# Layer step: the first two projection blocks loaded into tiles not yet in use, key gathers booked and issued differently, the sample's output rows laid out as 128 half rows

## The chip, the cores and the metric

One Trainium2 chip, one of its cores. The metric is the device time of one execution in microseconds (us), median of the runs shown. A profile of one execution lists what each engine did: PE (TensorE, the matmuls), DVE (VectorE), ACT (ScalarE), POOL (GpSimd), and SP, which here issues nearly all DMAs. Each engine works through its own queue in order.

## The reference

One decoder layer for a prompt of 256 tokens and for 8 sample requests of 8 tokens each, 320 rows in all, width 2048. One input projection feeds three branches: sparse attention over the top keys that an indexer chooses, a gated linear recurrence, and cross-attention into a memory.

```
z = einsum('btd,dn->btn', h, w)                      # 8272 columns, split into the branches' parts
dots = einsum('bthd,bld->bthl', iq, ik) * 64 ** -0.5     # 16 index heads of 64
sc = einsum('bth,bthl->btl', iw * 16 ** -0.5, relu(dots))
_, sel = top_k(where(causal, sc, -inf), n_sel)       # 64 keys (prompt) or 256 (sample)
a = softmax over the selected keys, times their values, times silu(gate)
y = layernorm(ALPHA * x + cat(a, b, m) @ w_out) * ln_g + ln_b
```

For the sample, past keys and values lie in pages (16 of 128 tokens per request, found through a page table): index keys `cache_idx_k`, keys `cache_k` and values `cache_v`.

## The kernel before

**Projection.** x stands transposed as 16 slabs (k) of 128 x 320. Every product is done at more than single precision: an operand is cast to a short format (`hi`, on ACT) and the remainder (`lo`, on DVE or POOL) is kept, and three matmuls are added: hi·hi, hi·lo, lo·hi. A block is 128 output columns: 48 matmuls of 320 columns into one PSUM tile `pj` (two buffers). The blocks come in the order of `PROJECTIONS`: `ikw` (the index key and head weights, 80 columns), eight `iq` (index queries, two heads each), eight `aq`, `ak`, `av`, then the rest. A weight block is loaded in two halves (list `wspec`; `half` counts them), each 128 x 1024 numbers, into the ring `wr` of three buffers (`load_w`); `prep` makes `wh` and `wl` of it (two buffers each); `pe_quantum` issues the matmuls, six per k. The blocks ikw and iq0 are cut into four parts each and taken in turns, ikw, iq0, ikw, iq0. x arrives in six loads (`load_x`, 2, 2, 2, 2, 4, 4 slabs) between those weights, and `split_x` makes `xh` and `xl`.

**After a block** its function empties the accumulator: `ev_ikw` (a DVE shuffle and multiplies with the rotary tables `tabi`, an ACT copy of the head weights), `ev_iq(i)` through `rope` (shuffle, multiply on DVE, a second multiply and an addition by `TT`). `TT` gives an operation to DVE or POOL, whichever the builder's clock says ends it earlier.

**Order of work.** A builder (`Plan`, `Engine`) keeps a clock for each engine and for the DMAs, with a cost for each operation, while it writes the program. The main loop asks that clock which weights to load, which operand to prepare, and whether PE gets a piece of projection, a page unit or a background step; each engine's queue is thereby fixed when the program is built. In `Plan.dma` a gather on POOL's queue costs 0.1 + 1.04 us, and other transfers run at 360 GB/s.

**Background steps.** `setup` loads `pidx` (row numbers), the page table and `tabi`, and makes `poff`. `idx_load` then gathers the index keys of all pages with 64 indirect DMAs on POOL, 16 for each of four groups of requests, into tiles tagged `pg`, `S`, `pg`, `S`; before every second one it waits until POOL is booked less than 0.5 us ahead. `idx_head` copies the eight new index keys per request (`nk`) on POOL. `idx_prompt` scores the prompt: for each iq block eight matmuls of 64 rows (`t,t` in the trace), relu on ACT, sums on DVE. `idx_sample` does the same for the sample with the gathered keys (from iq7 on), then `topk_sample` picks the keys in 32 rounds. `soft`, `unit` (page units: two requests, two pages each, of K or V), `hgrn`, `cross_prompt` and `split` follow. Page loads may start once `half` is over 38.

**End.** The output projection works on 512-column chunks n for row groups m = 0, 1 (prompt) and 2 (the 64 sample rows). `out_chunk` adds x and gathers row statistics, and after the last chunk `finish(m)` normalises: for each chunk subtract and multiply with g (DVE), then scale (ACT) and add b (POOL), or, for the sample's last two chunks, both in one DVE operation; two stores of 1024 columns.

Of the kernel before, what the change touches and what calls it, by code (L numbers as in the profile page):

```python
# [25 lines left out]
NS, NT = 64, 320  # L26
# [15 lines left out]
class Plan:  # L42
# [154 lines left out]
def hymba_step(ctx: ExitStack, tc: tile.TileContext, I, O):  # L197
# [95 lines left out]
    qpad = new([128, 8, 8, 32], "qpad")  # L293
# [76 lines left out]
    def ev_aq(h):  # L370
        def f(ps):
            x, sh = rope(ps, False)
            AQ[h] = T(256)
            r = h // 4 * 16 + h % 2 * 8
            TT(OP.add, qpad[:, :, h, r:r + 8], x[:, 256:320].rearrange("p (b t) -> p b t", b=8),
               sh[:, 256:320].rearrange("p (b t) -> p b t", b=8))
# [100 lines left out]
    def add_block(kind, i):  # L477
        nk = 4 if (kind, i) in (("ikw", 0), ("iq", 0)) else 8
        if kind == "ikw":
            add_T(I["wik"], ev_ikw, 80, nk)  # L480
        elif kind == "mem":
            for k in range(16):
                wspec.append(dict(kind="mem", k=k, n=1024, nq=1, src=I["wm"][:, k, :]))
        else:
            base, ev = {"iq": (32, ev_iq), "aq": (0, ev_aq), "ak": (8, ev_ak), "av": (16, ev_av), "mq": (56, ev_mq),
                        "bf": (44, None), "bq": (40, None), "bi": (48, None), "g": (24, None)}[kind]
            if kind == "g":
                add_T(wt[24 + i if i < 8 else 44 + i if i < 12 else 48 + i], ev_gate(i, i % 4 == 3))
            else:
                add_T(wt[base + i], ev(i) if ev else ev_b((kind, i)), nk=nk)  # L490
# [10 lines left out]
    wspec[0:8] = [wspec[4 * (i % 2) + i // 2] for i in range(8)]  # L501
# [37 lines left out]
    def load_w(i):  # L539
        s = wspec[i]  # L540
        WR[i] = new([128, 1024], "wr")
# [7 lines left out]
    def prep(i):  # L549
# [6 lines left out]
        if s.get("res") and kept.index(i) >= RES - 4:  # L556
# [5 lines left out]
            hi, lo = spare_w.pop(0), spare_w.pop(0)  # L562
        elif s.get("acc") == "rest":
# [5 lines left out]
        if i < 44:  # L569
# [34 lines left out]
    def unit(n):  # L604
        kind, p, u = punits[n]
        tl = [PG.pop((n, b)) for b in range(2)]
        if kind == "K":
# [5 lines left out]
            for hh in range(2):  # L613
                for h2 in range(2):
                    for b, hp, g in GROUPS:
                        h = 4 * hh + 2 * hp + h2
                        PE.matmul(st["kv"][g:g + 32, c:c + 256], qpad[:, 2 * p + b, h, :],
# [98 lines left out]
    def idx_head():  # L716
# [266 lines left out]
    def soft(p):  # L983
        yield from wait(("K", p), "topk", ("ak", 7), "masks")
        yield need(akS, qpad, ps=0)
# [4 lines left out]
        for hh in range(2):  # L990
            for h2 in range(2):
                for b, hp, g in GROUPS:
                    h = 4 * hh + 2 * hp + h2
                    PE.matmul(ps[g:g + 32, :], qpad[:, 2 * p + b, h, :], akS[:, h, :], start=hh == h2 == 0,
# [360 lines left out]
    def pe_quantum(i, q):  # L1355
# [5 lines left out]
        if s["kind"] == "T":  # L1361
# [106 lines left out]
    def out_chunk(n, ms, acc):  # L1468
        wait = acc == "main" and n in DEFER

        def f(o):
            c = slice(512 * n, 512 * n + 512)
            bn = st["bn"]
            for m, ps in zip(ms, o):
# [12 lines left out]
                r = st["r", 2][:, c]  # L1487
# [14 lines left out]
    def finish(m):  # L1502

        g, b = st["gb"]
        rows = 128 if m < 2 else 64
        r = st["r", m]
        s = T8()[0:rows]
        DVE.bn_aggr(out=s[:, 0:2], in_=st["bn"][0:rows, m])
        ACT.activation(s[:, 2:3], s[:, 1:2], AF.Sqrt, bias=eps[0:rows, 1:2])
        for c in range(4):  # L1510
            cs = slice(512 * c, 512 * c + 512)
            DVE.scalar_tensor_tensor(r[:, cs], r[:, cs], s[:, 0:1], g[0:rows, cs], op0=OP.subtract, op1=OP.mult)
            if c == 0:
                DVE.reciprocal(s[:, 2:3], s[:, 2:3])
            if m < 2 or c < 2:
                ACT.activation(r[:, cs], r[:, cs], AF.Copy, scale=s[:, 2:3])
                POOL.tensor_add(r[:, cs], r[:, cs], b[0:rows, cs])
            else:
                DVE.scalar_tensor_tensor(r[:, cs], r[:, cs], s[:, 2:3], b[0:rows, cs], op0=OP.mult, op1=OP.add)
            if c % 2:  # L1520
                SP.dma_start(O["y"][128 * m:128 * m + rows, 512 * c - 512:512 * c + 512],
                             r[:, 512 * c - 512:512 * c + 512])


    def load_x(k0, n, tag="pg"):
        t = new([128, n, NT], tag)
        SP.dma_start(t, I["xT"][:, k0:k0 + n, :])
        return k0, n, t

    def split_x(k0, n, t, mid=None):  # L1530
        for a in range(0, n, 2):
            if a and mid:
                mid()
            k = slice(k0 + a, k0 + a + 2)
            ACT.copy(xh[:, k, :], t[:, a:a + 2, :])
            DVE.tensor_sub(xl[:, k, :], t[:, a:a + 2, :], xh[:, k, :].bitcast(F32))
        free(t)

    load_w(0)
# [5 lines left out]
    first = [load_x(0, 2, "bp"), load_x(2, 2, "bp")]  # L1545
    load_w(1)
    first += [load_x(4, 2), load_x(6, 2)]
    load_w(2)
    prep(0)
    load_w(3)  # L1550
    split_x(*first[0])
    split_x(*first[1])
    first.append(load_x(8, 4))
    prep(1)
    load_w(4)
    split_x(*first[2])
    split_x(*first[3])
    first.append(load_x(12, 4))
    prep(2)
    load_w(5)  # L1560
    prep(3)
    split_x(*first[4], mid=lambda: prep(4))
    split_x(*first[5])
    first.clear()

    def setup():
        SP.dma_start(pidx, I["pidx"])
        SP.dma_start(ptab, I["pt"])
        for j in range(2):
            SP.dma_start(tabi[j], I["tabi"][:, j, :])  # L1570
# [12 lines left out]
        POOL.memset(qpad, 0.0)  # L1583
        POOL.memset(avS[0:64], 0.0)
# [4 lines left out]
        done.add("setup")  # L1589

# [32 lines left out]
    nw, npg, nunit, half, quarter, nprep = 6, 0, 0, 0, 0, 5  # L1623
# [23 lines left out]
    def loads():  # L1647
        nonlocal nw, npg
        while True:
# [16 lines left out]
            if (half > 38 and n < len(punits) and len(PG) + ("q" in st) + ci_live(0) < BUFS["pg"] and n <= nunit + 2  # L1666
# [30 lines left out]
    while half < len(wspec) or bg or outq or pending or nunit < len(punits):  # L1697
# [3 lines left out]
        while nprep < nw and nprep <= half + 1 + rest_next and prep_ready(nprep):  # L1701
# [143 lines left out]
```

## Time and profile before

| | before |
|---|---|
| median of 3 runs | 940.07 us (939.50 to 940.48) |
| the profiled execution's own time | 940.44 us |
| its span, first to last instruction | 938.7 us |
| mean granted TensorE clock | 0.984 |
| PE busy | 892.1 us, 95% |
| DMA traffic | 265.54 MB, mean 283 GB/s |
| index-key gathers on POOL | 64 (32 into `pg`, 32 into `S`) |

Line 127 is the one line in `Engine` through which nearly every operation is recorded, so groups are told apart by the tiles they write and read: `pj<-xh,wh` is a projection matmul, `wl<-wr,wh` a weight remainder, `t<-t,t` the work on rotated tiles, `pg<-in_ci,poff` a gather. A timeline row is: start, duration, engine, line, operation, output<-inputs, shapes, count, and in brackets the idle time before it with what ended it. A row of a table of windows is: the window, its length, then for PE, PEld (weight loads), DVE, ACT and POOL the busy time and in brackets the instructions, the granted clock, the DMA share and GB/s. In the list of waits a row is: who waited <- for whom: total us, times, longest.

### The profile page before, as it was taken

To read this page: it belongs to the slowest core of one execution; us is meant where nothing else is said; L and a number is where in the kernel's file an instruction comes from. 1 tells how busy PE (TensorE), PEld (TensorE's weight loads), DVE (VectorE), ACT (ScalarE), POOL (GpSimd) and SP (SyncE) were. 2 spreads that over 40 slices of the span, in tenths; PEclk is the share of its full clock that TensorE was granted. 3 is DMA by queue.
4 is the path that set the end of the run, shared out by engine and by line. 5 is a ranking of instruction groups with operands and counts; after the bars stand their busy time and mean duration, and the time that the engine had idled before them with its cause. 6 is when DMAs were issued, how large, how long until landed. Compare 5 with 4: busy or idle time off the path is not lost. (4 is left out here: it accounts for less than half of the span.)

```text
span 938.7 us, 18269 instructions
## 1 busy us (share of the span) xinstructions
PE 892.1 (95%) x6590; PEld 743.1 (79%) x6590; DVE 579.3 (62%) x1096; ACT 385.1 (41%) x673; POOL 299.8 (32%) x265
## 2 busy tenths in 40 slices
PE   8878899999999999999999999999999999999993
PEld 7777787888888888778888787777798878688872
DVE  5655799658899973376775763565444322645567
ACT  4322465644334344234354243444344332633333
POOL 1688783215565420032431231355100010011016
PEclk9999999999999999999999999999999999999997
DMA  8534443399899997997989989999898999945633
GB/s 257 190 117 157 125 128 120 96 343 372 273 375 348 361 360 271 406 347 287 365 330 339 408 311 376 402 342 400 320 326 322 358 353 404 303 143 155 202 113 112
DMA packets 79646, 265.54 MB, mean 283 GB/s; under 512 B 10050, under 2 KB 16899, under 8 KB 78979
## 3 DMA queue, kind: packets, MB, share of 16 engines
q1 hardware_dynamic: 77506, 260.17, 76.4%
q0 software_dynamic: 2048, 4.20, 1.5%
q8 instruction: 52, 0.85, 0.4%
q14 instruction: 40, 0.32, 0.1%
HBM read 255.60 MB, written 8.73 MB: 282 GB/s over the span
## 5 line engine op out<-in xcount | busy, mean ns | idle before, releaser
L127 PE MATMUL pj<-xh,wh 128*128 128x320 f32 (+1 forms) x1040 | 337.1, 324 | 6.7 <-ACT t L127 6.3
L127 PE MATMUL pj<-xh,wl 128*128 128x320 f32 (+1 forms) x1040 | 323.7, 311 | 1.8 <-DVE wl L127 1.8
L127 PE MATMUL pj<-xl,wh 128*128 128x320 f32 (+1 forms) x1040 | 323.8, 311 | 0.9 <-DVE xl L127 0.9
L127 DVE TENSOR_TENSOR wl<-wr,wh 128x1024 fp32r<-128x1024 f32 (+2 forms) x143 | 176.4, 1234 | 225.5 <-ACT wh L127 219.4
L127 ACT CAST wh<-wr 128x1024 fp32r<-128x1024 f32 (+2 forms) x178 | 181.7, 1022 | 237.2 <-PE pj L127 187.1
L127 PEld LDWEIGHTS pj<-xh,wh 128*128 128x128 f32 (+1 forms) x1040 | 197.0, 189 | 36.7 <-issue 25.9
L127 PEld LDWEIGHTS pj<-xh,wl 128*128 128x128 f32 (+1 forms) x1040 | 196.9, 189 | 3.0 <-DVE wl L127 2.9
L127 PEld LDWEIGHTS pj<-xl,wh 128*128 128x128 f32 (+1 forms) x1040 | 197.2, 190 | 2.5 <-DVE xl L127 1.4
L127 POOL TENSOR_TENSOR wl<-wr,wh 128x1024 fp32r<-128x1024 f32 x35 | 85.8, 2450 | 286.0 <-ACT wh L127 283.6
L127 POOL TENSOR_TENSOR t<-t,t 128x320 f32<-128x320 f32 (+4 forms) x74 | 66.0, 893 | 124.9 <-ACT t L127 89.9
L127 ACT ACTIVATE t<-t 128x320 f32<-128x320 f32 (+1 forms) x68 | 29.3, 455 | 79.5 <-DVE t L127 77.6
L127 PE MATMUL kv<-pg,qpad 128*32 128x256 f32 x1024 | 59.8, 381 | 0.0
L127 PE MATMUL va<-pg,PT 128*32 128x512 f32 x512 | 59.3, 596 | 0.0
L127 PEld LDWEIGHTS kv<-pg,qpad 128*32 128x32 f32 x1024 | 31.0, 110 | 23.0 <-issue 2.7
L127 POOL DMA_INDIRECT pg<-in_ci,poff x32 | 38.6, 1205 | 26.6 <-DMA t<-in_tabi 18.4
L127 DVE TENSOR_TENSOR t<-t,t 128x128 f32<-128x128 f32 (+5 forms) x50 | 23.9, 479 | 37.3 <-POOL t L127 21.8
L127 POOL DMA_INDIRECT S<-in_ci,poff x32 | 38.2, 1195 | 9.0 <-issue 8.4
L127 DVE MAX8 PT<-PT 128x8 f32<-128x1032 f32 x32 | 39.3, 1229 | 0.4
L127 DVE MATCH_REPLACE8 PT<-PT 128x1032 f32<-128x1032 f32 x32 | 39.0, 1218 | 0.0
L127 PEld LDWEIGHTS va<-pg,PT 128*32 128x32 f32 x512 | 14.5, 109 | 30.3 <-issue 27.8
L127 PE MATMUL mB<-t,t 128*128 128x64 f32 (+5 forms) x140 | 23.7, 328 | 9.9 <-DVE t L127 8.1
L127 POOL TENSOR_TENSOR t<-t,tabm 128x320 f32<-128x320 f32 x16 | 14.0, 876 | 56.2 <-DVE t L127 52.2
(294 smaller groups left out, 1240.2 us busy)
## 6 DMA issues: line engine op xcount, KB each, us to landing
pg<-in_ck SPq DMA_DIRECT2D x128, 512.0 KB
pg<-in_cv SPq DMA_DIRECT2D x128, 512.0 KB
wr<-in_wt SPq DMA_DIRECT2D x126, 512.0 KB
wr<-in_wo SPq DMA_DIRECT2D x36, 512.0 KB
wr<-in_wm SPq DMA_DIRECT2D x16, 512.0 KB
pg<-in_cXK SPq DMA_DIRECT2D x8, 512.0 KB
pg<-in_cXV SPq DMA_DIRECT2D x8, 512.0 KB
bp<-in_st SPq DMA_DIRECT2D x4, 512.0 KB
```

What stands on the lines that cost most here:

```text
L127: res = f(*a, **k)
```

## The change

The first two blocks are cut into eight parts each (two k, one part of six matmuls per turn), but loaded in four pieces each (four k) into parts of two tiles tagged `S`; their `hi` and `lo` go into the tiles tagged `PT`, `qpad`, `cat1` (`stacked`) and `pg`, all not otherwise used at that time. x comes as eight loads of two slabs into three `pg` tiles, in turns with the weights, and the two halves of iq1 are issued right behind; `tabi` is loaded before `pidx`. `qpad` is allocated and cleared, and `avS` cleared, only after iq0 is done. The builder's clock books a gather at 0.1 + 1.35 us and transfers at 270 GB/s up to 7 us and 375 afterwards; `idx_load` goes on when POOL is booked less than 1.5 us ahead. The eight `nk` copies move from POOL to ACT. Since the first blocks have eight more parts, the counts 38 and 44 become 46 and 52. For the sample, rows 0 to 63 of a 128 x 1024 tile hold the first 1024 columns and rows 64 to 127 the other 1024, with g and b loaded to match; statistics of the upper half are copied down, mean and factor copied up, and four DVE operations and four stores do what six DVE, two ACT and two POOL operations and two stores did.

```diff
         else:
-            self.t[q] = t + 1.04
+            self.t[q] = t + 1.35
             t += 2.6
-        self.t["DMA"] = end = max(self.t["DMA"], t) + nbytes / 360e3
+        self.t["DMA"] = end = max(self.t["DMA"], t, 0.9) + nbytes / (375e3 if t > 7 else 270e3)
...
-    qpad = new([128, 8, 8, 32], "qpad")
...
-        nk = 4 if (kind, i) in (("ikw", 0), ("iq", 0)) else 8
+        nk = 2 if (kind, i) in (("ikw", 0), ("iq", 0)) else 8
...
-    wspec[0:8] = [wspec[4 * (i % 2) + i // 2] for i in range(8)]
+    wspec[0:16] = [wspec[8 * (i % 2) + i // 2] for i in range(16)]
...
-        WR[i] = new([128, 1024], "wr")
+        WR[i] = s["home"] if "home" in s else new([128, 1024], "wr")
...
+        elif "pair" in s:
+            hi, lo = s["pair"]
...
-        if i < 44:
+        if i < 52:
             DVE.tensor_sub(lo[:, 0:n], raw[:, 0:n], hi[:, 0:n].bitcast(F32))
...
-                    yield from idle("POOL", 0.5)
+                    yield from idle("POOL", 1.5)
...
-                    POOL.tensor_copy(nk[64 * j:64 * j + 64, 8 * a:8 * a + 8],
+                    ACT.copy(nk[64 * j:64 * j + 64, 8 * a:8 * a + 8],
                                      ik[64 * j:64 * j + 64, 256 + 8 * b:264 + 8 * b])
...
-                PE.matmul(ps, h3[:, k, :], xh[:, K, :], start=K == 0, stop=False)
-                PE.matmul(ps, h3[:, k, :], xl[:, K, :], start=False, stop=False)
-                PE.matmul(ps, l3[:, k, :], xh[:, K, :], start=False, stop=K == 15)
+                j = k + s.get("sub", 0)
+                PE.matmul(ps, h3[:, j, :], xh[:, K, :], start=K == 0, stop=False)
+                PE.matmul(ps, h3[:, j, :], xl[:, K, :], start=False, stop=False)
+                PE.matmul(ps, l3[:, j, :], xh[:, K, :], start=False, stop=K == 15)
...
-        rows = 128 if m < 2 else 64
-        r = new([128, 2048], "S" if m < 2 else "pg")[0:rows]
-        SP.dma_start(r, I["xn"][128 * m:128 * m + rows, :])
-        st["r", m] = r
+        if m < 2:
+            st["r", m] = r = new([128, 2048], "S")
+            SP.dma_start(r, I["xn"][128 * m:128 * m + 128, :])
+        else:
+            st["r", 2] = r = new([128, 1024], "pg")
+            st["gb2"] = gb = new([128, 2, 1024], "pg")
+            for h in range(2):
+                rows, cols = slice(64 * h, 64 * h + 64), slice(1024 * h, 1024 * h + 1024)
+                SP.dma_start(r[rows], I["xn"][256:320, cols])
+                for j, n in enumerate(("lng", "lnb")):
+                    SP.dma_start(gb[rows, j, :], bass.AP(tensor=I[n].tensor, offset=I[n].offset + 1024 * h,
+                                                         ap=[[0, 64], [1, 1024]]))
...
-                r = st["r", 2][:, c]
+                rows = slice(64 * (n // 2), 64 * (n // 2) + 64)
+                r = st["r", 2][rows, 512 * (n % 2):512 * (n % 2) + 512]
                 DVE.scalar_tensor_tensor(r, r, ALPHA, ps[0:64], op0=OP.mult, op1=OP.add)
                 DVE.tensor_add(r, r, ps[64:128])
                 if acc == "rest":
                     DVE.tensor_add(r, r, part(n))
-                DVE.bn_stats(out=bn[0:64, 2, n, :], in_=r)
+                DVE.bn_stats(out=bn[rows, 2, n, :], in_=r)
                 if n == 3:
-                    finish(2)
+                    finish_sample()
...
-            if m < 2 or c < 2:
-                ACT.activation(r[:, cs], r[:, cs], AF.Copy, scale=s[:, 2:3])
-                POOL.tensor_add(r[:, cs], r[:, cs], b[0:rows, cs])
-            else:
-                DVE.scalar_tensor_tensor(r[:, cs], r[:, cs], s[:, 2:3], b[0:rows, cs], op0=OP.mult, op1=OP.add)
+            ACT.activation(r[:, cs], r[:, cs], AF.Copy, scale=s[:, 2:3])
+            POOL.tensor_add(r[:, cs], r[:, cs], b[:, cs])
...
+    def finish_sample():
+        r, gb, bn, s = st["r", 2], st["gb2"], st["bn"], T8()
+        DVE.tensor_copy(bn[0:64, 2, 2:4, :], bn[64:128, 2, 2:4, :])
+        DVE.bn_aggr(out=s[0:64, 0:2], in_=bn[0:64, 2])
+        ACT.activation(s[0:64, 2:3], s[0:64, 1:2], AF.Sqrt, bias=eps[0:64, 1:2])
+        DVE.tensor_copy(s[64:128, 0:1], s[0:64, 0:1])
+        for c in range(2):
+            cs = slice(512 * c, 512 * c + 512)
+            DVE.scalar_tensor_tensor(r[:, cs], r[:, cs], s[:, 0:1], gb[:, 0, cs], op0=OP.subtract, op1=OP.mult)
+            if c == 0:
+                DVE.reciprocal(s[0:64, 2:3], s[0:64, 2:3])
+                DVE.tensor_copy(s[64:128, 2:3], s[0:64, 2:3])
+        for c in range(2):
+            cs = slice(512 * c, 512 * c + 512)
+            DVE.scalar_tensor_tensor(r[:, cs], r[:, cs], s[:, 2:3], gb[:, 1, cs], op0=OP.mult, op1=OP.add)
+            for h in range(2):
+                SP.dma_start(O["y"][256:320, 1024 * h + 512 * c:1024 * h + 512 * c + 512], r[64 * h:64 * h + 64, cs])
+    raws = [new([128, 1280], "S"), new([128, 2048], "S")]
+    his = [new([128, 2320], "PT", F32R), new([128, 2048], "qpad", F32R)]
+    los = [stacked, new([128, 2048], "pg", F32R)]
+    xs = [new([128, 6, NT], "pg") for _ in range(3)]
+    plan.split.update(t.tensor.name for t in raws + his + los + xs)
+    for i in range(16):
+        w = (320, 512)[i % 2]
+        c = slice(w * (i // 4), w * (i // 4 + 1))
+        wspec[i].update(n=w, home=raws[i % 2][:, c], pair=(his[i % 2][:, c], los[i % 2][:, c]), sub=i // 2 % 2 * 2)
+    def load_first(i):
+        k = slice(4 * (i // 4), 4 * (i // 4) + 4)
+        src = (I["wik"], wt[32])[i % 2][:, k, :]
+        WR[i] = wspec[i]["home"]
+        SP.dma_start(WR[i], src.rearrange("p a c -> p (a c)"))
+    def prep_first(i):
+        prep(i)
+        WH[i + 2], WL[i + 2] = WH[i], WL[i]
+    def x_pair(a):
+        return xs[a // 3][:, 2 * (a % 3):2 * (a % 3) + 2, :]
+    def load_x(a):
+        SP.dma_start(x_pair(a), I["xT"][:, 2 * a:2 * a + 2, :])
+    def split_x(a):
+        k = slice(2 * a, 2 * a + 2)
+        ACT.copy(xh[:, k, :], x_pair(a))
+        DVE.tensor_sub(xl[:, k, :], x_pair(a), xh[:, k, :].bitcast(F32))
...
+    for q in range(4):
+        if q:
+            load_first(4 * q)
+        load_x(2 * q)
+        load_first(4 * q + 1)
+        load_x(2 * q + 1)
+    load_w(16)
+    load_w(17)
+    for q in range(4):
+        prep_first(4 * q)
+        split_x(2 * q)
+        prep_first(4 * q + 1)
+        split_x(2 * q + 1)
...
+        for j in range(2):
+            SP.dma_start(tabi[j], I["tabi"][:, j, :])
         SP.dma_start(pidx, I["pidx"])
         SP.dma_start(ptab, I["pt"])
-        for j in range(2):
-            SP.dma_start(tabi[j], I["tabi"][:, j, :])
...
-        POOL.memset(qpad, 0.0)
-        POOL.memset(avS[0:64], 0.0)
         POOL.memset(onesm, 1.0 / 128)
         POOL.memset(one, 1.0)
         POOL.memset(eps[:, 0:1], RMS_EPS)
         POOL.memset(eps[:, 1:2], LN_EPS)
         done.add("setup")
+        yield from wait(("iq", 0))
+        st["qpad"] = new([128, 8, 8, 32], "qpad")
+        POOL.memset(st["qpad"], 0.0)
+        POOL.memset(avS[0:64], 0.0)
...
-    nw, npg, nunit, half, quarter, nprep = 6, 0, 0, 0, 0, 5
+    nw, npg, nunit, half, quarter, nprep = 18, 0, 0, 0, 0, 16
...
-            if (half > 38 and n < len(punits) and len(PG) + ("q" in st) + ci_live(0) < BUFS["pg"] and n <= nunit + 2
+            if (half > 46 and n < len(punits) and len(PG) + ("q" in st) + ci_live(0) < BUFS["pg"] and n <= nunit + 2
...
-        while nprep < nw and nprep <= half + 1 + rest_next and prep_ready(nprep):
+        while nprep < nw and nprep <= half + 1 + rest_next + 2 * (half < 16) and prep_ready(nprep):
```

More of the change, by code (lines that the diff above doesn't have):

```diff
@@ L374, in f @@
             r = h // 4 * 16 + h % 2 * 8
-            TT(OP.add, qpad[:, :, h, r:r + 8], x[:, 256:320].rearrange("p (b t) -> p b t", b=8),
+            TT(OP.add, st["qpad"][:, :, h, r:r + 8], x[:, 256:320].rearrange("p (b t) -> p b t", b=8),
                sh[:, 256:320].rearrange("p (b t) -> p b t", b=8))
@@ L616, in unit @@
                         h = 4 * hh + 2 * hp + h2
-                        PE.matmul(st["kv"][g:g + 32, c:c + 256], qpad[:, 2 * p + b, h, :],
+                        PE.matmul(st["kv"][g:g + 32, c:c + 256], st["qpad"][:, 2 * p + b, h, :],
                                   tl[b][:, :, 128 * h:128 * h + 128], start=hh == h2 == 0, stop=hh == h2 == 1)
@@ L984, in soft @@
         yield from wait(("K", p), "topk", ("ak", 7), "masks")
-        yield need(akS, qpad, ps=0)
+        yield need(akS, st["qpad"], ps=0)
         while "kv" in st or plan.slot_free("kv", 1) > plan.now:
@@ L993, in soft @@
                     h = 4 * hh + 2 * hp + h2
-                    PE.matmul(ps[g:g + 32, :], qpad[:, 2 * p + b, h, :], akS[:, h, :], start=hh == h2 == 0,
+                    PE.matmul(ps[g:g + 32, :], st["qpad"][:, 2 * p + b, h, :], akS[:, h, :], start=hh == h2 == 0,
                               stop=hh == h2 == 1)
@@ L1504, in finish @@
         g, b = st["gb"]
-        rows = 128 if m < 2 else 64
         r = st["r", m]
-        s = T8()[0:rows]
-        DVE.bn_aggr(out=s[:, 0:2], in_=st["bn"][0:rows, m])
-        ACT.activation(s[:, 2:3], s[:, 1:2], AF.Sqrt, bias=eps[0:rows, 1:2])
+        s = T8()
+        DVE.bn_aggr(out=s[:, 0:2], in_=st["bn"][:, m])
+        ACT.activation(s[:, 2:3], s[:, 1:2], AF.Sqrt, bias=eps[:, 1:2])
         for c in range(4):
             cs = slice(512 * c, 512 * c + 512)
-            DVE.scalar_tensor_tensor(r[:, cs], r[:, cs], s[:, 0:1], g[0:rows, cs], op0=OP.subtract, op1=OP.mult)
+            DVE.scalar_tensor_tensor(r[:, cs], r[:, cs], s[:, 0:1], g[:, cs], op0=OP.subtract, op1=OP.mult)
@@ L1520, in finish @@
             if c % 2:
-                SP.dma_start(O["y"][128 * m:128 * m + rows, 512 * c - 512:512 * c + 512],
+                SP.dma_start(O["y"][128 * m:128 * m + 128, 512 * c - 512:512 * c + 512],
                              r[:, 512 * c - 512:512 * c + 512])
[L1525 to L1537, printed above, removed]
@@ L1540, in hymba_step @@
+    load_first(0)
     warm, warm_ps = T(256, BF), PS([128, 256], "kv")
@@ L1544, in hymba_step @@
     free(warm)
[L1545 to L1564, printed above, removed]
+    for q in range(4):
[11 more added lines that the diff above has]
+        split_x(2 * q + 1)
     def setup():
+        for j in range(2):
+            SP.dma_start(tabi[j], I["tabi"][:, j, :])
         SP.dma_start(pidx, I["pidx"])
         SP.dma_start(ptab, I["pt"])
-        for j in range(2):
-            SP.dma_start(tabi[j], I["tabi"][:, j, :])
         yield need(pidx)
```

1 line of the change is left out of this document (removed).

## The prediction

> **What bounds the kernel now.** I read the page's engine shares first, then its forty slices, then the list of PE's waits (30 us in all), then the timeline around the longest.
>
> ```profile
> PE 892.1 (95%) x6590; PEld 743.1 (79%) x6590; DVE 579.3 (62%) x1096; ACT 385.1 (41%) x673; POOL 299.8 (32%) x265
> PE   8878899999999999999999999999999999999993
> POOL 1688783215565420032431231355100010011016
> DMA  8534443399899997997989989999898999945633
> ```
>
> TensorE is the bound: 95% overall, nines from the sixth slice to the last but one. What is not nine is the first five slices (about 117 us), where POOL stands at 6 to 8 from the second on, and the last slice. So I looked for PE's waits there: every row below is a matmul group with the idle time before it in brackets.
>
> ```profile
> 22.96 0.31 PE L127 MATMUL pj<-xh,wl 128*128 128x320 f32 x1
> 27.61 0.41 PE L127 MATMUL pj<-xh,wh 128*128 128x320 f32 x1 [4.33 <-ACT t L127]
> 55.83 1.65 PE L127 MATMUL mB<-t,t 64*128 64x128 f32 x8 [4.21 <-DVE t L127]
> 65.97 0.93 PE L127 MATMUL mA<-t,t 64*128 64x128 f32 x8 [0.49 <-issue]
> 75.85 0.93 PE L127 MATMUL mB<-t,t 64*128 64x128 f32 x8 [1.72 <-DVE t L127]
> 85.73 0.93 PE L127 MATMUL mA<-t,t 64*128 64x128 f32 x8 [1.72 <-DVE t L127]
> 95.61 0.93 PE L127 MATMUL mB<-t,t 64*128 64x128 f32 x8 [1.73 <-DVE t L127]
> ```
>
> Two kinds of stall. At 23.1 PE has finished the first two projection blocks (ikw, iq0) and waits 4.33 us until an ACT copy has emptied the ikw accumulator. Then each index-score step (`idx_prompt`, the `t,t` matmuls of 64 rows) waits for its rotated queries: 4.21 + 0.49 + 1.72 + 1.72 + 1.73 = 9.9 us. They come 9.88 us apart from 65.97 on, a fixed beat, so something other than PE sets it. POOL and DVE in one beat:
>
> ```profile
> 65.52 1.15 POOL L127 DMA_INDIRECT S<-in_ci,poff  x1 [0.16 <-issue]
> 66.97 1.75 POOL L127 DMA_INDIRECT S<-in_ci,poff  x1 [0.30 <-issue]
> ...
> 73.41 0.94 POOL L127 DMA_INDIRECT S<-in_ci,poff  x1 [0.30 <-issue]
> 74.36 0.88 POOL L127 TENSOR_TENSOR t<-t,t 128x320 f32<-128x320 f32 x1
> ...
> 75.28 0.42 DVE L127 TENSOR_TENSOR t<-t,t 128x256 f32<-128x256 f32 x1 [3.42 <-POOL t L127]
> ```
>
> Six gathers fill 65.52 to 74.35, 1.47 us each; behind them in POOL's queue stands the rope's multiply, DVE waits 3.42 us for it, PE for DVE. The builder books a gather at 0.1 + 1.04 = 1.14 us, so it believes POOL free long before it is. The clock makes stalls dearer (last columns but two: granted clock, DMA share, GB/s):
>
> ```profile
> 0.00:5.00 5.00, 3.93 (x21) 2.70 (x21) 0.73 (x3) 2.46 (x3) 0.34 (x5) 1.00 0.63 187
> 5.00:10.00 5.00, 3.70 (x20) 2.60 (x20) 2.85 (x4) 2.59 (x4) 0.00 (x0) 1.00 1.00 326
> 10.00:15.00 5.00, 4.73 (x33) 4.43 (x32) 3.80 (x7) 3.02 (x6) 0.00 (x0) 1.00 0.83 279
> 28.40:31.80 3.40, 3.40 (x15) 3.40 (x14) 2.59 (x7) 0.22 (x1) 1.25 (x2) 0.50 0.55 158
> 98.00:100.00 2.00, 2.00 (x10) 2.00 (x9) 0.87 (x3) 0.31 (x1) 1.39 (x3) 0.50 0.66 172
> ```
>
> After three of the stalls the granted clock is 0.50: by the starts in the timeline a 320-column matmul then takes 0.267 us instead of the usual 0.147. That cost about 1.45 us after 28.4 (12 matmuls), 1.55 after 96.5 (13), and 1.3 after 55.83, whose group took 1.65 us instead of 0.93.
>
> **Part 1, the start.** All of x, ikw and iq0 (2.62 + 0.66 + 1.05 = 4.33 MB, from the shapes) is now issued at once, into tiles that need no release. Before, SP held weight loads for the three-deep ring and the DMA share sank to 0.83. By 5 us 0.94 MB have moved (187 GB/s in the first window); the other 3.39 MB at the 326 of the row above end at 15.4. I allow 1.5 us until they can be read (x for k 8 to 11 was read at 12.14, when about 0.35 MB more than needed had moved: 1.2). Then comes x's last pair: ACT cast, DVE difference, 11 matmuls.
>
> ```profile
> 4.17 0.72 ACT L127 CAST xh<-bp 128x640 fp32r<-128x640 f32 x1 [0.64 <-DMA bp<-in_xT]
> 4.92 0.82 DVE L127 TENSOR_TENSOR xl<-bp,xh 128x640 fp32r<-128x640 f32 x1 [0.88 <-ACT xh L127]
> 23.83 1.04 ACT L127 CAST wh<-wr 128x1024 fp32r<-128x1024 f32 x1 [3.55 <-DMA wr<-in_wt]
> 24.90 1.22 DVE L127 TENSOR_TENSOR wl<-wr,wh 128x1024 fp32r<-128x1024 f32 x1 [3.90 <-ACT wh L127]
> 27.14 0.42 ACT L127 COPY t<-pj 16x320 f32<-16x320 f32 x1 [2.26 <-DVE t L127]
> ```
>
> 16.9 + 0.72 + 0.82 + 11 x 0.147 = 20.1 for the end of the two blocks, 3 us earlier. But `pj` has two buffers, so iq1 still waits for ikw's emptying, and that needs tabi, which now queues behind iq1's two weight halves: they are usable at 18.5 and 20.1 (0.52 MB, 1.6 us each), tabi at 21.1. DVE is in order; I expect both halves' differences ahead of the shuffle: 20.1 + 1.04 + 1.22 = 22.4. From there to PE it was 26.12 to 27.61, 1.5 us. So iq1 starts near 23.9 instead of 27.61: **-3.7** (ends: 21.6, if the shuffle comes first and tabi early; 26.3, if transfers run like the 279 row). The stall is still 3.8 us, so I keep the 1.45 us at half clock.
>
> On that stall, the Trainium skill (TensorE: Matmul & The Clock Gate, Part 1: The HAM clock gate) ties half clock to an idle window of about 3.4 us. The trace is harsher: 1.73 us of waiting at 95.61 was enough once and 1.72 at 85.73 was not. By the page a stall cut below its window would save 1.45 us more.
>
> The same skill speaks against the smaller loads (DMA: Bandwidth & Descriptors, Rules for kernel authors: at least 1 MiB per DMA for full bandwidth). Here loads of 160 to 320 KB kept the DMA share at 1.00 in the 5 to 10 row. If the rule held and the 279 of the next row applied, everything up to tabi would come 2.4 us later and this part would give -1.3.
>
> **Part 2, gathers and copies.** A gather is now booked at 1.45 us, close to the measured 1.47, and two more are issued only while POOL is booked less than 1.5 us ahead. A beat of PE is 48 x 0.147 + 0.93 = 8.0 us, so 5.5 gathers per beat, 8.1 us. The rope's multiply goes to DVE when POOL is booked further ahead (about 0.5 us by the 0.42 of a 256-column one, hidden in the 3.42 that DVE now waits), or to POOL with its queue known. Either way the matmul is placed where the operand is truly there. The eight key copies leave POOL and its queue, the qpad memset enters it later:
>
> ```profile
> 46.62 2.70 POOL L127 COPY nk<-t 64x8 f32<-64x8 f32 x7 [3.01 <-issue]
> 21.82 1.83 POOL L127 MEMSET qpad<- 128x2048 f32 x1
> 160.68 0.15 DVE L127 COPY PT<-va 128x8 f32<-128x8 f32 x1
> 160.87 1.83 DVE L127 TENSOR_TENSOR cat<-S,cat 64x512 fp32r<-64x512 f32 x2
> ```
>
> No row shows such a copy on ACT. Eight by the 0.42 copy of 16 x 320 above are 3.4 us, by 0.39 each on POOL 3.1; fewer columns speak for less, down to 0. They wait for DVE's sum, and behind them on ACT stand the next score relu and the next weight cast; weights are cast half a block ahead (24 x 0.147 = 3.5 us of PE), so I take 0 on the path, 1 at worst. The memset now waits until iq0's matmuls have left its tile; behind it in POOL's queue wait only gathers, 1.83 us later, and the builder books it. Of 9.9 us of waits and 2.85 us of half clock after them I expect 2 us to stay, as gathers start later (pidx is now behind tabi and its DVE work behind the ikw emptying: about 26 instead of 19.4): **-11.0** (ends 0 and -13). They finish near 26 + 64 x 1.47 + 3 = 123; DVE first read the last group's keys at 160.87, so even 15 us earlier they are there.
>
> **Part 3, sample rows at the end.**
>
> ```profile
> 922.88 5.72 POOL L127 TENSOR_TENSOR S<-S,pg 128x512 f32<-128x512 f32 x4 [1.46 <-ACT S L127]
> 922.59 1.09 PE L127 MATMUL pj<-pg,qpad 128*128 128x512 f32 x4
> 927.11 0.26 DVE L127 BATCH_NORM_AGGREGATE s<-bn 64x2 f32<-64x24 f32 x1
> 927.40 1.75 DVE L127 SCALAR_TENSOR_TENSOR pg<-pg,s,pg 64x512 f32<-64x512 f32 x1
> 929.15 5.50 DVE L127 SCALAR_TENSOR_TENSOR pg<-pg,s,pg 64x512 f32<-64x512 f32 x5
> 933.35 1.80 SPq L127 DMA_DIRECT2D out_y<-pg  x2
> ```
>
> and, from the chain of work that ended last, its last piece:
>
> ```profile
> 933.91 0.74 DVE pg L127
> ```
>
> PE's last group starts at 922.59 and is done at 923.7; DVE carries the end. Six passes over 64 x 512 run from 927.40 to 934.65, slowed beside POOL's adds (1.75, then 1.10 each, against 0.74 for the last, when POOL is through). Now there are four on 128 rows and no POOL in them. Three tiny copies come in; the nearest row is the 128x8 copy at 160.68, 0.15 us, which I take (0 to 0.5). Statistics 927.1 + 0.15 + 0.27 + 0.15; the first pass still stands beside POOL's last add (to 928.6) and ends as before at 929.15; reciprocal and copy to 929.4; three passes of 0.74 to 931.6. From the last pass to the end of the span it was 938.7 - 934.65 = 4.05; a second store adds one issue, about 0.45 (1.80 for two with a wait between): 936.1. **-2.6** (ends -1.6 and -3.2). The extra loads for this (1.05 MB, five more issues) fall after 800 us, where the DMA slices show one 9 and then 3 to 6: 0, or 3.2 us if the weights had no lead.
>
> **The middle.** The builder lays out the order against its own clock, so all of it changes somewhat; page loads start at the same block (38 + 8 = 46), and 200 to 800 us holds only a handful of waits (largest 2.80). I take 0, plus or minus 6.
>
> **Sum.** -3.7 - 11.0 - 2.6 = -17.3 on the profiled execution's 940.44 us (span 938.7): 923.1. The median of the runs is 0.4 lower, so **923 us**; own range 914 to 931.
>
> **Rivals.**
> *POOL stays the bound.* Gathers take 0.94 or about 1.75 us; the long ones may stand beside DVE work, and DVE gets more. With four long ones in 5.5, a beat takes 5.5 x 1.25 + 4 x 0.8 = 10 us, as now. Then part 2 gives nothing: 934. For it: both lengths are in the rows; against: PE waits only if an operand of its own is behind them. 0.14.
> *The start is hidden anyway*, iq1 held to 27 by tabi and the DVE order: 926.7; inside my range, 0.1 of the forecast's chance.
> *Slower: pages come later than booked.* The builder now books transfers at 375 GB/s instead of 360.
>
> ```profile
> 200.00:400.00 200.00, 196.89 (x1723) 168.50 (x1722) 152.06 (x254) 77.61 (x146) 72.20 (x40) 0.99 0.94 350
> ```
>
> A page unit is four loads of 128 x 1024 numbers, 2.1 MB: 5.6 us booked, 6.0 at 350. If PE, no longer late itself, had to wait that 0.4 us in each of 64 units, 26 us would be lost: 949. It eats the gain from 0.27 us per unit, that is below 357 GB/s. Against it: 350 was at a share of 0.94, so 372 when full, and PE never waited for a page. 0.07.
> *More than forecast*, no stall left at iq1 and a better middle: below 914, 0.07.
>
> **Chances.** Forecast 0.72, the others as given. Range 911 to 935: it leaves out the slow rival and the best cases. A difference under 0.2% is about what cannot be told from none: faster 0.91, same 0.02, slower 0.07.
>
> **What would show it.** iq1's first matmul near 24; `t,t` matmuls about 8.1 us apart with under 0.5 us before them; about five gathers per beat; six DVE passes become four, the end 4.5 us after the last. It is wrong if PE shows waits on page loads, if the beat stays at 9.9, or if iq1 still starts after 26.

## The result, and the profile after

After the change the median is **924.17 us** (923.53 to 924.95, 4 runs) against 940.28 us for the kernel before (939.50 to 941.08, 4 runs): ratio 0.9829, 95% interval 0.9812 to 0.9846. The forecast was 923.0, range 911 to 935. The profiled execution took 924.32 us; its span is 922.5 us.

The page of the kernel after, shares and slices, the same rows as before:

```profile
PE 888.3 (96%) x6588; PEld 740.6 (80%) x6590; DVE 576.2 (62%) x1099; ACT 383.2 (42%) x675; POOL 300.5 (33%) x257
PE   8999999999999999999999999999899999899994
POOL 0776868444744541332311311355100000011015
DMA  8544436889999936999989989999994999844643
```

The holes in PE's slices 2 to 5 are closed; two new eights stand late in the row (slices 29 and 35; the first holds a wait of 2.96 us at 657.86, where the kernel before waited 1.93). PE's busy time fell by 3.8 us only: nearly all that was won is waiting.

Timeline of PE in the kernel after, the end of the two first blocks, iq1's first matmul, and the last four index-score steps:

```profile
21.46 0.31 PE L127 MATMUL pj<-xh,pg 128*128 128x320 f32 x1
22.48 0.42 PE L127 MATMUL pj<-xh,wh 128*128 128x320 f32 x1 [0.71 <-ACT t L127]
...
61.07 0.93 PE L127 MATMUL mB<-t,t 64*128 64x128 f32 x8
...
69.16 0.93 PE L127 MATMUL mA<-t,t 64*128 64x128 f32 x8
...
77.24 0.93 PE L127 MATMUL mB<-t,t 64*128 64x128 f32 x8
...
85.33 0.93 PE L127 MATMUL mA<-t,t 64*128 64x128 f32 x8
```

iq1 starts at 22.48 instead of 27.61 after a wait of 0.71 us, and the score steps stand 8.08 us apart with no bracket at all: PE waits for none of them. POOL in one beat of the kernel after:

```profile
67.75 1.17 POOL L127 DMA_INDIRECT S<-in_ci,poff  x1
69.23 1.74 POOL L127 DMA_INDIRECT S<-in_ci,poff  x1 [0.31 <-issue]
71.28 0.98 POOL L127 DMA_INDIRECT S<-in_ci,poff  x1 [0.30 <-issue]
72.56 0.94 POOL L127 DMA_INDIRECT S<-in_ci,poff  x1 [0.30 <-issue]
74.85 0.88 POOL L127 TENSOR_TENSOR t<-t,t 128x320 f32<-128x320 f32 x1 [1.34 <-DVE t L127]
```

Four gathers, then POOL is idle for 1.34 us until DVE hands it the rope's multiply. Before, six gathers stood ahead of it and DVE waited 3.42 us. The waiting has changed sides.

One stall is new. PE, ACT and SP of the kernel after, around the switch to the output weights (first loads of `in_wo` into the ring):

```profile
804.23 0.66 PE L127 MATMUL mA<-wh,xh 128*128 128x512 f32 x1 [2.96 <-ACT wh L127]
```

```profile
803.13 1.04 ACT L127 CAST wh<-wr 128x1024 fp32r<-128x1024 f32 x1 [6.68 <-DMA wr<-in_wo]
```

```profile
785.85 0.54 SPq L127 DMA_DIRECT2D pg<-in_xn  x1
786.44 0.59 SPq L127 DMA_DIRECT2D pg<-in_lng  x1
...
790.31 0.38 SPq L127 DMA_DIRECT2D pg<-in_lnb  x1
791.03 3.53 SPq L127 DMA_DIRECT2D wr<-in_wo  x2
```

From 785.85 to 790.69 SP issues eight loads of x rows, g and b (the kernel before has three there); the weights queue behind them, the cast waits 6.68 us for one, PE 2.96 us for the cast. From 790 to 795 us the DMA engines are full (share 1.04) but move only 215 GB/s; from 795 to 800, with weights, it is 362. And the tail, DVE in the kernel after:

```profile
913.60 0.17 DVE L127 COPY bn<-bn 64x12 f32<-64x12 f32 x1
913.81 0.25 DVE L127 BATCH_NORM_AGGREGATE s<-bn 64x2 f32<-64x24 f32 x1
...
914.28 1.23 DVE L127 SCALAR_TENSOR_TENSOR pg<-pg,s,pg 128x512 f32<-128x512 f32 x1
...
915.79 2.08 DVE L127 SCALAR_TENSOR_TENSOR pg<-pg,s,pg 128x512 f32<-128x512 f32 x3
```

Four passes in place of six, 0.69 us each once POOL is through; 128 rows cost what 64 did. Read at five points of PE's timeline (us), the account is:

| | before | after | gained in the stage |
|---|---|---|---|
| iq1's first matmul | 27.61 | 22.48 | 5.1 |
| last index-score step | 105.58 | 85.33 | 15.1 |
| last projection matmul | 798.25 | 782.90 | -4.9 |
| PE's last group ends | 923.68 | 909.98 | -1.6 |
| end of the span | 938.7 | 922.5 | 2.5 |

So 22.7 us were won at the start, in the score steps and at the very end, and 6.5 given back between the last score step and PE's last group.

### The profile page after: what moved, and what is told of

Read it like the earlier page. It is cut to its first block, busy times and chain, and to the rows that moved or that the text cites. A ratio compares the mean times of both kernels' runs of the same rounds, so it can differ in the third digit from the quotient of the medians.

```text
span 922.5 us, 18247 instructions
## 1 busy us (share of the span) xinstructions
PE 888.3 (96%) x6588; PEld 740.6 (80%) x6590; DVE 576.2 (62%) x1099; ACT 383.2 (42%) x675; POOL 300.5 (33%) x257
## 5 line engine op out<-in xcount | busy, mean ns | idle before, releaser
L127 PE MATMUL pj<-xh,wh 128*128 128x320 f32 x1008 | 325.2, 323 | 3.7 <-ACT t L127 3.7
L127 PE MATMUL pj<-xh,wl 128*128 128x320 f32 x1008 | 312.0, 310 | 1.2 <-POOL wl L127 1.1
L127 PE MATMUL pj<-xl,wh 128*128 128x320 f32 x1008 | 312.1, 310 | 0.0
L127 DVE TENSOR_TENSOR wl<-wr,wh 128x1024 fp32r<-128x1024 f32 x133 | 168.4, 1267 | 211.2 <-ACT wh L127 205.4
L127 ACT CAST wh<-wr 128x1024 fp32r<-128x1024 f32 x170 | 177.8, 1046 | 242.1 <-PE pj L127 197.5
L127 PEld LDWEIGHTS pj<-xh,wh 128*128 128x128 f32 x1008 | 190.2, 189 | 33.1 <-issue 24.9
L127 POOL TENSOR_TENSOR wl<-wr,wh 128x1024 fp32r<-128x1024 f32 x37 | 91.1, 2465 | 321.5 <-ACT wh L127 308.0
L127 PEld LDWEIGHTS pj<-xh,wl 128*128 128x128 f32 x1008 | 190.0, 189 | 1.9 <-POOL wl L127 1.4
L127 PEld LDWEIGHTS pj<-xl,wh 128*128 128x128 f32 x1008 | 190.4, 189 | 1.2
L127 PE MATMUL mB<-t,wh 128*128 128x256 f32 x128 | 25.8, 295 | 1.8 <-POOL t L127 1.7
```

The source lines that it names most:

```text
L127: res = f(*a, **k)
```

## The experiments

Theory: the start gives its lead, the booking of the gathers frees PE in the score steps, the tail gives 2.5 us, and the extra loads at the end cost about 4.6. Rivals: POOL is the bound and swallows the start; the gain comes from another part than its name says (copies, margin, transfer rate); the given-back time is page loads. "Lost time" below is PE's time over the common pitch of each kind of matmul, added up from the rows of its timeline in a stage. Behind each time stand, in brackets, its ratio to the kernel before as timed in the same series (medians 939.93, 940.36 and 940.50 us) and the 95% interval of that ratio. Times within a run are those of its one profiled execution.

**Part 1 alone.** The kernel after with booking, margin, copies and tail of before:

```diff
-            self.t[q] = t + 1.35
+            self.t[q] = t + 1.04
-                    yield from idle("POOL", 1.5)
+                    yield from idle("POOL", 0.5)
-                    ACT.copy(nk[
+                    POOL.tensor_copy(nk[
```

> The new start alone (first two blocks in unused tiles, x in eight loads, qpad cleared later, transfers booked at 270 and 375 GB/s); gathers booked and spaced as before, key copies on POOL, sample rows as before. Theory 'the parts add': iq1's first matmul near 22.5 us as in the changed kernel (27.61 before) and no half clock after it, so 5.1 + 1.5 us less: about 933.7 us; index-score steps still 9.9 us apart with waits of 1.7 us. Rival 'POOL swallows the start': the gathers now begin 7 us later and are still booked too short, so POOL is late by that much more and the last index-score step comes at about 105 us as before: about 940 us.

Measured 943.84 us against 939.93 (1.0046, 1.0029 to 1.0062): alone, the new start makes the kernel slower. iq1 stands at 22.21, so its lead is there, but the last step comes at 98.09, 7.5 us earlier than before, and the beat is back:

```profile
49.63 1.65 PE L127 MATMUL mB<-t,t 64*128 64x128 f32 x8 [4.93 <-DVE t L127]
...
78.31 0.93 PE L127 MATMUL mA<-t,t 64*128 64x128 f32 x8 [1.73 <-DVE t L127]
...
88.19 0.93 PE L127 MATMUL mB<-t,t 64*128 64x128 f32 x8 [1.73 <-DVE t L127]
```

Neither theory's number. POOL does set the beat, and the 7.5 us were lost later, with 3 more. Most of that shows in one window, before first, then this kernel (columns as in the tables of windows; the first bracketed figure's time is PE's):

```profile
200.00:340.00 140.00, 137.03 (x1219) 119.92 (x1218) 127.56 (x209) 54.33 (x110) 71.84 (x39) 0.99 0.95 352
```

```profile
200.00:340.00 140.00, 131.37 (x1220) 111.90 (x1213) 129.41 (x203) 49.97 (x101) 70.80 (x38) 0.98 0.94 354
```

PE is busy 131.4 of 140 us instead of 137.0. This window became the second question of the study.

**Part 2 alone.** The kernel before with the three lines above turned the other way.

> The gather part alone (booked at 0.1 + 1.35 us, issued while POOL is booked less than 1.5 us ahead, the eight key copies on ACT); start and sample rows as before. Theory 'the parts add': the score steps come 8.1 us apart without waits, 13.7 us less than before: about 926.6 us, iq1 still at 27.6. Rival 'only together with the later start': the gathers begin at 19 us, ahead of the clearing of qpad, and part of the waits stays: 932 us or more.

Measured 929.95 us (0.9894, 0.9878 to 0.9911). The steps come 8.1 us apart (one 9.0) without a wait and the last stands at 91.14, 14.4 us earlier than before; 2.9 are given back in the middle. This part does what its name says, whatever the start does.

**Parts 1 and 2, tail of before.**

> The kernel after with the tail of before: the first two parts of the change alone. If the parts add, it has the kernel after's order up to the output weights, no stall at 804 us (4.6 less) and the old tail (2.5 more): 922. Rival, the builder's order in the middle shifts as in the runs of one part alone, by 3 to 10 us: 926 to 934.

Measured 922.59 us (0.9797, 0.9763 to 0.9831), as the sum said. There is no stall behind 800 us (0.7 us lost between 790 and 830, after 5.3).

**Part 3 alone.** The kernel before with the new tail and its loads.

> The sample rows' new layout alone (128 half rows, extra loads of g and b), the rest as before. Theory 'the extra loads stall PE': the end after PE's last matmul is 12.5 us instead of 15.0, but the 1.05 MB more, issued in one row ahead of output weights, hold those weights back and PE waits 3 us and then runs at half clock, 4.6 us together: about 942.4 us. Rival 'that stall has nothing to do with the loads': no such wait at 800 to 825 us: about 937.8 us.

Measured 944.01 us (1.0047, 1.0030 to 1.0064), 4.1 slower. From PE's last group to the end it is 12.6 us instead of 15.0, but the stall came with it:

```profile
822.31 0.50 PE L127 MATMUL mA<-wh,xh 128*128 128x512 f32 x1 [3.60 <-ACT wh L127]
```

Between 790 and 830 PE lost 7.4 us, before 0.8.

**The new tail without its extra loads.** g and b are loaded whole anyway; POOL copies the halves:

```diff
-                for j, n in enumerate(("lng", "lnb")):
-                    SP.dma_start(gb[rows, j, :], ...)
...
+            for j in range(2):
+                for h in range(2):
+                    POOL.tensor_copy(st["gb2"][rows, j, :], gb[j][rows, cols])
```

> The changed kernel with g and b for the half rows copied on POOL from the tiles that are loaded anyway, so that the four extra loads (1.05 MB) go. Theory 'the extra loads stall PE': the wait of 2.96 us at 804 us and the half clock after it are gone: about 919.6 us. Rival 'transfers are booked too fast' (375 GB/s) or any other cause: the wait at 804 stays: 924 us.

Measured **920.05 us** (0.9782, 0.9765 to 0.9799): the best version, and its interval does not touch that of the kernel after. The stall is gone (0.8 us lost between 790 and 830). So the loads make the stall, not the tail's arithmetic. The other traces agree: in all eight kernels that have the extra loads PE has such a wait, of 2.75 to 3.94 us, between 804 and 826 us, and in the six without them it has none.

**Which line of part 2 carries it.** Three runs undo one line each in the kernel after. First the copies:

> The changed kernel with the eight key copies put back on POOL. They are booked at 0.14 us and took 0.39 each, and POOL stood idle 3 us ahead of them before. Theory 'they add one wait': POOL is 2 to 5 us late once, one wait of that size before an early t,t matmul and perhaps half clock after it: 926 to 929 us. Rival 'POOL has room for them now': no wait, 924 us.

Measured 928.96 us (0.9898, 0.9865 to 0.9930): one wait of 3.02 us at 55.79 returns. Then the booking:

> The changed kernel with the gather's booking alone put back (0.1 + 1.04 us; still issued up to 1.5 us ahead, key copies still on ACT). Theory 'the booking is what removed the waits': six or seven gathers per score step again, beat 9.9 us or more, waits before the t,t matmuls back, about 11 us more: 935 us. Rival 'the copies and the margin did it': beat near 8.1 us, 924 to 927 us.

Measured 941.30 us (1.0014, 0.9994 to 1.0033; ten runs, 938.36 to 946.38, the profiled one the longest): the whole gain is gone, more than was expected. The beat is back at 9.9 us:

```profile
75.13 0.93 PE L127 MATMUL mA<-t,t 64*128 64x128 f32 x8 [1.73 <-DVE t L127]
...
85.02 0.93 PE L127 MATMUL mB<-t,t 64*128 64x128 f32 x8 [1.74 <-DVE t L127]
```

The last step comes 9.75 us later than in the kernel after; as much again is lost before the last projection matmul (803.59 against 782.90), for the most part between 200 and 340 us (PE busy 131.65 us there, after 138.37). The longer waits there are those of the run with part 1 alone, one for one (2.69, 1.15 and 2.57 us against 2.71, 1.15 and 2.58), though that run had the old margin and copies too. So what part 1 lost in the middle goes with the old booking under the new start. Then the margin:

> The changed kernel with the margin alone put back (gathers issued only while POOL is booked less than 0.5 us ahead). Theory 'the booking is what removed the waits': with true costs the margin decides little, beat 8.1 us, no waits before the t,t matmuls: 924 us, 3 more or less by the order in the middle. Rival 'it is the wider spacing': the waits return, 930 us or more.

Measured 946.52 us (1.0067, 1.0043 to 1.0091), and the beat has no part in it: there the theory held, the steps are as in the kernel after, four gathers between them, the last at 85.11. All 22 us are lost later. The last gather, in the kernel after and then in this one:

```profile
166.33 0.94 POOL L127 DMA_INDIRECT S<-in_ci,poff  x1 [0.30 <-issue]
```

```profile
190.35 0.95 POOL L127 DMA_INDIRECT S<-in_ci,poff  x1 [0.30 <-issue]
```

24 us later. With it everything moves that needs the gathered keys: the first of the 32 selection rounds from 210.23 to 233.97, the first matmul with the mask from 337.38 to 365.52.

**The transfer rate.**

> The changed kernel with transfers booked at 360 GB/s throughout, as before. Theory 'the booked rate does nothing for the start': iq1 still near 22.5 us, beat 8.1 us; the order of the middle differs, 924 us with 4 more or less. Rival 'the 375 GB/s cost the middle its 4 us': fewer waits between 120 and 790 us, 920 us.

Measured 933.07 us (0.9915, 0.9886 to 0.9944). Start and beat are nearly unchanged (iq1 22.95, last step 85.81), though the edit takes back the early 270 GB/s and the floor of 0.9 us too, and the gathers begin at 21.76 instead of 27.03. Between 200 and 340 us PE is busy 132.4 us instead of 138.4, and nearly all of that is one wait:

```profile
338.64 0.61 PE L127 MATMUL mA<-maskb,emat 128*128 128x512 bf16 x1 [5.51 <-DVE maskb L127]
```

The mask is hardly later than in the kernel after (DVE ends it at 338.59, there at 336.50); there PE has other work until 337.38. With the booking and with the margin turned back PE waits at the same place, 2.57 and 4.09 us. Some 4 of the 9 us are lost before the last projection matmul, the rest behind it. That last stage, up to PE's last group, falls into four cases over all fourteen traces: 122.5 to 123.1 us with the new rates and no extra loads, 125.4 with the old rate and none, 127.1 to 128.6 with the new rates and the loads, 131.2 to 131.6 with the old rate and the loads. So the booked rates are worth some 9 us to this kernel, all of it through the order that the builder lays out.

**Is it the late selection?** The late mask named a mechanism for the middle: 32 rounds of 2.5 us on DVE that start after the last gather. Half of them left out, once with margin 0.5 and once in the kernel after:

```diff
+        DVE.memset(L[:, 128:256], FLOOR)
-        for r in range(32):
+        for r in range(16):
```

> The kernel after with the gathers held back as before (margin 0.5), as in the run that took 946.5 us, and with 16 rounds of the sample's top 256 instead of 32: it leaves out half of that selection (the rest of the list is filled with the floor), so its mask is another one. In the run with margin 0.5 the last gather came at 190.35 us and not at 166.33, the rounds began at 233.97 and not at 210.23, and the first product with the mask stood at 365.52 and not at 337.38. Theory, the late selection is what cost the 20 us: 16 rounds less take 16 x (1.23 + 0.09 + 1.22) = 41 us out of VectorE's chain, the mask is there by 325 to 335, and the time is 920 to 932. Rival, the gathers' place changed the order of the pages and weights, and the mask only shows it: 940 or more.

> The kernel after itself with 16 rounds of the sample's top 256 instead of 32 (half of that selection is left out). Control for the run with the margin. Theory, in the kernel after the selection is no longer what the end waits for, apart from the waits around 330 to 350 us: TensorE lost 8.5 us between 200 and 340 us, a part of it comes back, 916 to 924. If the selection bounds the kernel after as well, the 41 us less move the mask to about 300 and the time falls below 912.

Measured 938.82 us (0.9976, 0.9959 to 0.9994) and 925.75 us (0.9830, 0.9797 to 0.9863). With the margin, the mask came at 318.13 instead of 365.52 and 7.7 of the 22 us came back. In the kernel after, the mask came at 293.60 instead of 337.38 and nothing came back. Both times lie outside what was expected of them. So the late selection is about a third of that loss, as far as these runs can tell (16 rounds fewer are booked as well, so the builder's order changes with them), in the kernel after it bounds nothing, and my theory of the middle falls for the greater part. What stays open is the larger part. With the margin and half the rounds PE is busy 131.36 us between 200 and 340 (138.37 in the kernel after); its waits of over 1 us there are 2.09 and 1.05 for `cat`, 1.17 for another DVE result and 1.83 for the mask, and one of 6.34 us stands at 675.54, where the kernel after waits 2.96. Which decision of the builder makes these places, these runs do not tell.

**More gathers ahead.** The best version with margin 3.0:

> The version with the scale and shift rows copied on POOL (920.05 us), with the gathers' margin 3.0 instead of 1.5, so that more gathers go ahead of each head's products on POOL. Theory, the selection starts earlier but nothing waits for it, so nothing is won: 919 to 923. If the earlier selection is still worth its lead, the mask comes 5 us or more sooner and the time falls below 917. Rival, POOL becomes the bound of the beat again, waits ahead of the score steps return: 925 or more.

Measured **973.59 us** (1.0340, 1.0306 to 1.0374), far outside every theory. 42 gathers now stand in one row on POOL, from 32.96 to 86 us. PE, then ACT of this kernel, in the midst of them:

```profile
78.03 0.43 PE L127 MATMUL pj<-xh,wh 128*128 128x320 f32 x1 [2.37 <-issue]
80.83 0.43 PE L127 MATMUL pj<-xl,wh 128*128 128x320 f32 x1 [2.37 <-issue]
83.64 0.43 PE L127 MATMUL pj<-xh,wl 128*128 128x320 f32 x1 [2.37 <-issue]
```

```profile
90.65 1.05 ACT L127 CAST wh<-wr 128x1024 fp32r<-128x1024 f32 x1 [41.77 <-remote]
```

The brackets name neither an engine nor a load. The windows of this kernel before, in and behind the row of gathers:

```profile
30.00:40.00 10.00, 10.00 (x73) 8.93 (x72) 6.61 (x20) 4.04 (x12) 8.31 (x10) 1.00 0.56 189
...
70.00:80.00 10.00, 1.71 (x4) 1.15 (x4) 0.00 (x0) 0.00 (x0) 7.56 (x8) 0.50 0.20 53
...
100.00:110.00 10.00, 10.00 (x72) 9.31 (x69) 7.96 (x20) 3.85 (x6) 0.00 (x0) 1.00 0.34 107
```

Four matmuls in 10 us instead of 72, DVE and ACT at nought, the DMA engines a fifth busy, the clock at half. The DMA queues of this kernel from 43 to 86 us (packets, MB, share):

```profile
q0 software_dynamic: 1088, 2.23, 19.0%
q1 hardware_dynamic: 144, 0.52, 3.7%
q14 instruction: 1, 0.01, 0.1%
```

One instruction packet moved in 43 us; in the kernel after, in the same 43 us, there were four (two in each of two queues) and 1576 packets of ordinary loads. The engines seem to run out of instructions while the gathers follow each other 0.30 us apart; that fits the rows, but no run isolates it, and it is not shown.

## Why the prediction was right, and where it was not

**Part 1, -3.7: measured -5.1, and the 1.45 us of half clock behind it went too.** The order that I chose, both halves' differences ahead of the shuffle, is what happened (DVE's two differences end at 20.99, the shuffle starts at 21.03, ACT copies at 22.01). Two sizes were off. Loads ran faster than the row that I used:

```profile
10.00:15.00 5.00, 5.00 (x36) 5.00 (x35) 4.78 (x8) 4.20 (x8) 0.00 (x0) 1.00 1.05 391
15.00:20.00 5.00, 5.00 (x36) 5.00 (x35) 4.04 (x6) 3.73 (x5) 0.00 (x0) 1.00 0.97 366
20.00:25.00 5.00, 4.29 (x30) 4.03 (x29) 4.23 (x11) 0.42 (x1) 0.96 (x2) 1.00 0.69 238
```

391 and 366 GB/s in place of 326 (kernel after). And PE has 5.00 of 5 us of work there: from 10 us on it was PE itself that set the end of the two blocks, 21.6 and not 20.1. I had let the last x pair set it. So, with the differences done 1.4 us sooner too, the stall behind them was 0.71 and not 3.8 us, and no half clock followed: the granted clock is 1.00 in all three rows. That a short wait is safe is not shown: in the profile of the version that copies on POOL, whose start is the same, a wait of 0.81 us at 7.65 was followed by some 3.4 us of half clock, and iq1 came at 23.69; the kernel after has a wait of 0.80 us there and no half clock behind it.

**Part 2, -11.0: measured -13.7** (15.1 less the 1.45 that belong to the start), a little beyond the end that I gave as -13. The 2 us that I let stay did not stay. The beat of 8.1 us came true, though with four gathers in it and not 5.5: I had divided the beat by a gather's price, as if POOL were full, and left out that the multiply stays on POOL and waits there 1.34 us for DVE. So the gathers ended at 167 and not at 123 (146 before), and the first selection round began at 210.23, 2 us later than before, though the last score step came 20 us sooner; that 24 us more are too many is what the run with margin 0.5 shows. Eight copies on ACT took 1.64 us, 0.2 each, below the rows that I took for them.

**Part 3, -2.6: measured -2.5.** The three small copies took 0.15 to 0.17 us as the nearest row said, the passes 0.69.

**The failed step** is the one on that part's extra loads: that they "fall after 800 us" where the DMA slices sink, and so cost 0, "or 3.2 us if the weights had no lead". They were issued from 785.85 on, ahead of the output weights in SP's queue, and cost 4.1 to 4.5 us: 4.1 by the medians with and without them, 4.2 by the time from the last projection matmul to PE's last group (127.08 us, in the version that copies 122.89), 4.5 by the lost time there. I had read the slices rightly, but the loads fell into the one with the 9 (the 35th begins at 784 in the kernel after) and not behind it, and the place in the queue was not looked up.

**The middle, 0 plus or minus 6: about 2 us lost** (the 6.5 less the 4.5 of the stall). Inside the bound, but the bound was luck. Turning back one line moved the time from the last score step to PE's last group by 8 to 22 us in the runs above (rate 8.1, booking 12.4, margin 22.2).

So each gain came by the way that was forecast, but that the time was right to 1.2 us is luck: 5.5 us won at start and beat beyond the forecast (20.2 less 14.7) nearly made up for the 6.5 lost to stall and middle. Of the rivals, POOL as the bound is what the kernel is without the booking (the run with 1.04), and pages that come late did not show: no wait of PE for a page load stands in the list of the kernel after, and taking back the rate that I feared costs 9 us.

The Trainium skill (TensorE: Matmul & The Clock Gate, Part 1: The HAM clock gate) ties half clock to an idle window of about 3.4 us. The measurement decides against it again: behind the wait of 2.96 us at 804 the granted clock of the kernel after fell to 0.72 in a window of five:

```profile
805.00:810.00 5.00, 4.82 (x16) 3.65 (x16) 4.60 (x17) 3.41 (x16) 0.00 (x0) 0.72 0.62 190
```

Nor does the length of a wait alone decide it: in the same kernel waits of 1.43 us (at 171.19) and 1.79 us (at 510.12) were followed by a granted clock of 0.50, waits of 1.76 us (at 429.98) and 2.10 us (at 471.06) were not.

The Trainium skill's rule of at least 1 MiB per DMA for full bandwidth (DMA: Bandwidth & Descriptors, Rules for kernel authors) is not borne out by the start's loads of 160 to 320 KB, which moved at 391 GB/s from 10 to 15 us. The row of 5 to 10 us that I read for it in the kernel before did not hold such loads alone: one of 640 KB was among them.

## What to carry to other kernels

Where a builder lays out the order against its own clock, a wrong price for one operation shows as waits of another engine at a fixed beat; correct the price from the trace first: turning that one line back cost 17 us here (924 to 941). A faster start is not won time until the last stage has it: here its lead stood through the score steps (7.5 us at the last) and was lost, with 3 us more, in the order that the old price laid out behind them. Before a load is called free, look up what stands behind it in its queue.

## What the runs showed of the hardware

A row of 42 gathers 0.30 us apart went with a near halt of the other engines for some 40 us (973.6 us, clock 0.50, waits that name no engine), while rows of four to six with other work between did not; the cause is open. A DVE pass over 512 columns took the same 0.69 to 0.74 us on 128 rows as on 64. Gathers of 0.94 and of up to 1.75 us stand side by side on POOL in the score steps, and the prediction's guess that the long ones stand beside DVE work is borne out: in all fourteen traces no gather without DVE work beside it took more than 1.00 us, and every one over 1.5 us had DVE work beside it for more than half of its time. But DVE work does not always lengthen one: in each trace 7 to 18 gathers took at most 0.96 us with DVE busy nearly throughout.
